# A quadrant swap in DRAM: 16 DMA engines that work on 16 neighbouring rows, or on rows 17 apart

## The chip, the cores and the metric

The kernel runs on one core of a Trainium2 chip. The time is that of the device for one execution, in microseconds (us). The input lies in DRAM, the output goes to DRAM, and both have 8192 x 8192 float32 elements, 268.44 MB each.

## The reference

```python
def reference(x: np.ndarray) -> np.ndarray:
    return np.fft.ifftshift(x)
```

With 8192 rows and columns this swaps quadrants. Output row r, column c is input row (r + 4096) mod 8192, column (c + 4096) mod 8192. Nothing is calculated: each half row of the output (4096 elements, 16 KB) is one contiguous half row of the input.

## The kernel before, in words

The kernel consists of DMAs from DRAM to DRAM and nothing else. No tile in on-chip memory is used, and no compute engine takes part. A DMA here is an instruction on one of two queues: that of SyncE (SP, `nc.sync`) and that of ScalarE (ACT, `nc.scalar`). It is described by three dimensions, the first of which has 16 entries, one for each of the core's 16 DMA engines (`ENGINES`, L9). In what follows "engine" means one of these 16.

`copy` (L26 to L32) issues one DMA. Its dimensions are `[[C, 16], [16 * C, 16], [1, hc]]`: engine e starts at row `row + e` and then takes every sixteenth row, 16 rows in all, half a row (16 KB) at a time. A row is 32 KB long, so at any moment the 16 engines are set to work on 16 neighbouring rows, 32 KB apart, and each engine goes on in steps of 512 KB. One DMA moves 256 half rows, 4 MB.

The loop (L35 to L38) goes over the rows in 32 blocks of 256. In each block SP's queue copies one half of the rows and ACT's queue the other half. Which half is SP's alternates from block to block. So each queue has 32 DMAs, and the two queues carry equal bytes. The program itself contains no wait between DMAs. Those that the profile shows are put in by the layer that turns the program into instructions.

Of the kernel before, what the change touches and what calls it, by code (L numbers as in the profile page):

```python
# [1 line left out]

# [4 lines left out]


ENGINES = 16  # L9


@with_exitstack
def kernel(
    ctx: ExitStack,
    tc: tile.TileContext,
    x: bass.AP,
    out: bass.AP,
):
    nc = tc.nc
    R, C = x.shape  # L20
    hr = R // 2
    hc = C // 2
    per = 16
    rows = ENGINES * per

    def copy(queue, row, h, step):  # L26

        dims = [[C, ENGINES], [step * C, per], [1, hc]]
        queue.dma_start(
            out=bass.AP(out.tensor, out.offset + row * C + h, dims),  # L30
            in_=bass.AP(x.tensor, x.offset + (row + hr) % R * C + hc - h, dims),
        )  # L32


    for n, row in enumerate(range(0, R, rows)):  # L35
        left = n % 2 == 0
        copy(nc.sync, row, 0 if left else hc, ENGINES)
        copy(nc.scalar, row, hc if left else 0, ENGINES)  # L38


# [1 line left out]
_INS = ['x']  # L42
_OUTS = [((8192, 8192), 'float32')]


def kernel(**inputs):
    import numpy as _np
    import concourse.bacc as _bacc
    import concourse.tile as _tile
    from concourse import mybir as _mybir  # L50
    from concourse.bass_utils import run_bass_kernel_spmd as _run

    nc = _bacc.Bacc("TRN2", target_bir_lowering=False, num_devices=1)  # L53
    arrays, args = {}, []
    for name in _INS:
        a = _np.ascontiguousarray(inputs[name])
        if a.dtype.kind in "iu":
            a = a.astype(_np.int64)
        arrays[f"in_{name}_dram"] = a
        args.append(nc.dram_tensor(f"in_{name}_dram", a.shape, _mybir.dt.from_np(a.dtype), kind="ExternalInput").ap())  # L60
    for i, (shape, dtype) in enumerate(_OUTS):
        dt = _mybir.dt.from_np(_np.dtype(dtype))
        args.append(nc.dram_tensor(f"out_{i}_dram", shape, dt, kind="ExternalOutput").ap())
    with _tile.TileContext(nc) as tc:
        kernel(tc, *args)
    r = _run(nc, [arrays], core_ids=[0])
    got = tuple(r.results[0][f"out_{i}_dram"] for i in range(len(_OUTS)))
    return got[0]
```

## Time and profile before

| What | Value |
|---|---|
| Median of 3 runs | 813.71 us (813.11 to 814.12) |
| Profiled execution: span from the first to the last instruction | 813.2 us |
| DMA issues, each of 4096 KB | 32 on SP's queue, 32 on ACT's |
| One issue on ACT's queue, min/median/max | 578 / 578 / 882 ns |
| One issue on SP's queue, min/median/max | 571 / 571 / 786 ns |
| From issue to landing, min/median/max | 25.3 / 101.1 / 104.6 us |
| Rate of reading in 100 to 800 us | 332 GB/s |

The profile covers one execution, and its span stands for the device time: 813.2 us lies inside the range of the three runs and 0.5 us from their median. The rate counts each byte once, though each is both read and written. The page counts packets, which are the single transfers an engine makes: 16,384 of them are half rows, and the 1,024 under 512 B are the 16 that each of the 64 DMAs ends with, one for each engine. "Share" in the table of queues is the time that the packets of a queue took, out of 16 engines for the whole span.

### The profile page before, as it was taken

The numbers are of one execution on the slowest core, as the hardware profiler recorded it, in microseconds if no ns is written. First come the engines' busy times: TensorE is split into PE (matmuls) and PEld (weight loads), VectorE is DVE, ScalarE is ACT, GpSimd is POOL, SyncE is SP. The second block draws the span as 40 slices with busy tenths as digits, with TensorE's granted clock in tenths as the row PEclk, the third lists the DMA queues.
The fourth block names the chain that finished last, engine by engine and source line by source line (L and its number), as shares of the span: only waits on it lengthen the run. The fifth ranks groups of instructions, "written<-read, shape, count | busy, mean of one in ns | idle before, by whom it ended". The sixth has DMA issues, their size and how long they took to land. (4 is left out here: it accounts for less than half of the span.)

```text
span 813.2 us, 109 instructions
## 1 busy us (share of the span) xinstructions
POOL 0.2 (0%) x4
## 2 busy tenths in 40 slices
POOL 0000000000000000000000000000000000000000
DMA  9999999999999999999999999999999999999998
GB/s 303 336 326 331 334 329 323 330 338 333 330 333 330 334 334 330 335 334 330 325 338 330 336 330 334 334 333 331 341 331 330 334 334 330 333 328 336 331 334 276
DMA packets 17408, 268.44 MB, mean 330 GB/s; under 512 B 1024, under 2 KB 1024, under 8 KB 1024
## 3 DMA queue, kind: packets, MB, share of 16 engines
q1 hardware_dynamic: 8704, 134.22, 50.4%
q10 hardware_dynamic: 8704, 134.22, 48.6%
HBM read 268.44 MB, written 268.44 MB: 660 GB/s over the span
## 5 line engine op out<-in xcount | busy, mean ns | idle before, releaser
L53 POOL MEMSET const-bfloat16-1.0<- 128x1 bf16 x1 | 0.1, 102 | 0.0
L53 POOL MEMSET const-uint8-127<- 128x1 uint8 x1 | 0.1, 101 | 0.0
L53 POOL MEMSET const-float32-0.0<- 128x1 f32 x1 | 0.1, 99 | 0.2 <-issue 0.2
L53 POOL MEMSET const-float32-1.0<- 128x1 f32 x1 | 0.1, 98 | 0.0
## 6 DMA issues: line engine op xcount, KB each, us to landing
out_dram<-in_x_dram SPq DMA_DIRECT2D x32, 4096.0 KB, 101.2
out_dram<-in_x_dram ACTq DMA_DIRECT2D x32, 4096.0 KB, 101.1
```

What stands on the lines that cost most here:

```text
L53: nc = _bacc.Bacc("TRN2", target_bir_lowering=False, num_devices=1)
```

## The change

The rows are cut into four parts: the upper and the lower 4096 rows, each with the left and the right half of the columns. In each part, SP's queue now copies a slanted band. Engine e starts 17 rows behind engine e - 1 in memory order (`(ENGINES + 1) * C`) and again walks in steps of 16 rows. So at each step the engines stand 17 rows (544 KB) apart, where they stood one row apart. A band takes 241 steps of 16 rows each (`last` = 4096 / 16 - 15). It is cut into seven DMAs of 32 steps and one of 17. That makes 32 DMAs on SP's queue: 28 of 8 MB and 4 of 4.25 MB.

The band leaves a triangle of rows at the start and at the end of each part, 120 half rows each. ACT's queue copies these. A DMA takes n neighbouring half rows (n from 1 to 15) and cuts each into 16 strips of 256 elements (1 KB), one for each engine. The DMAs of start and end alternate, with 15 - m and m + 1 half rows. So each pair has 16 half rows, and each part has 15 pairs. That makes 120 DMAs with 960 half rows (15.73 MB) and 960 strips for each engine.

In the program, all 32 DMAs of SP's queue are written first, and then all 120 of ACT's.

```diff
-    per = 16
-    rows = ENGINES * per
-
-    def copy(queue, row, h, step):
-
-        dims = [[C, ENGINES], [step * C, per], [1, hc]]
+    def copy(queue, row, col, dims):
         queue.dma_start(
-            out=bass.AP(out.tensor, out.offset + row * C + h, dims),
-            in_=bass.AP(x.tensor, x.offset + (row + hr) % R * C + hc - h, dims),
+            out=bass.AP(out.tensor, out.offset + row * C + col, dims),
+            in_=bass.AP(x.tensor, x.offset + (row + hr) % R * C + (col + hc) % C, dims),
         )
-    for n, row in enumerate(range(0, R, rows)):
-        left = n % 2 == 0
-        copy(nc.sync, row, 0 if left else hc, ENGINES)
-        copy(nc.scalar, row, hc if left else 0, ENGINES)
+    steps = 32
+    ahead = ENGINES - 1
+    strip = hc // ENGINES
+    last = hr // ENGINES - ahead
+    parts = [(row, h) for h in (0, hc) for row in (0, hr)]
+
+    for begin, h in parts:
+        for at in range(0, last, steps):
+            n = min(steps, last - at)
+            copy(
+                nc.sync,
+                begin + ENGINES * at,
+                h,
+                [[(ENGINES + 1) * C, ENGINES], [ENGINES * C, n], [1, hc]],
+            )
+
+    for begin, h in parts:
+        for m in range(ahead):
+            for row, n in (
+                (ENGINES * m + m + 1, ahead - m),
+                (ENGINES * (last + m), m + 1),
+            ):
+                copy(nc.scalar, begin + row, h, [[strip, ENGINES], [C, n], [1, strip]])
```

## The prediction

> **What bounds the kernel now.** I read the page first: the slices of the span, then the queues. There is nothing but DMA in it.
>
> ```profile
> span 813.2 us, 109 instructions
> DMA  9999999999999999999999999999999999999998
> GB/s 303 336 326 331 334 329 323 330 338 333 330 333 330 334 334 330 335 334 330 325 338 330 336 330 334 334 333 331 341 331 330 334 334 330 333 328 336 331 334 276
> DMA packets 17408, 268.44 MB, mean 330 GB/s; under 512 B 1024, under 2 KB 1024, under 8 KB 1024
> HBM read 268.44 MB, written 268.44 MB: 660 GB/s over the span
> ```
>
> The 16 engines are busy in every slice, and except in the first and the last the rate stays between 323 and 341 GB/s. So no wait of the program sets the time, only the rate at which bytes move. A half row takes 0.786 us on an engine: the queues' shares, 50.4% and 48.6%, are 99.0% of 16 x 813.2 us, over 16,384 half rows. Next I read the same view for the stretch from 100 to 800 us, to have the rate without start and end:
>
> ```profile
> DMA packets 15092, 232.59 MB, mean 332 GB/s; under 512 B 896, under 2 KB 896, under 8 KB 896
> q1 hardware_dynamic: 7545, 116.28, 50.7%
> q10 hardware_dynamic: 7547, 116.31, 49.0%
> ```
>
> At 332 GB/s, 268.44 MB take 808.6 us. The other 4.6 us are the start (nothing moves in the first 2 us) and the end (20 GB/s in the last 3.2 us). 808.6 + 4.6 = 813.2 us, the whole span. I work against this span; the median of the runs is 0.5 us more.
>
> Two more views tell how DMAs are kept in flight: the waits of SP's queue, and the landings of the instructions on the line that issues.
>
> ```profile
> SPq L29 <- DMA out_dram<-in_x_dram: 689.7, 28, 25.1
> ...
> L29 SPq DMA_DIRECT2D out_dram<-in_x_dram x32: 571/571/786, 0.7 to 709.0; - x32
> L29 ACTq DMA_DIRECT2D out_dram<-in_x_dram x32: 578/578/882, 0.7 to 713.9; - x32
> ...
> DMA to landing us min/median/max: 25.3/101.1/104.6
> ```
>
> Of SP's 32 DMAs, 28 wait for an earlier DMA: four go out at once, then one every 25 us. A landing after 101.1 us is four times that interval, so four are in flight on each queue and eight on both. An issue costs its queue 0.57 to 0.88 us. Eight in flight is plenty here, since the queues wait with 75 us of work in hand.
>
> **The change part by part.**
>
> *Rows 17 apart in place of 1.* The bytes are the same, and so is the size of SP's packets. What might change is how the DRAM takes them, and nothing in this trace shows rows 17 apart. The nearest rows bound it. At the fastest slice, 341 GB/s, 268.44 MB would take 787 us, and at the slowest inner one, 323, they would take 831 us. The queues give another hint. q1 and q10 carry the same packets, but q1's take 50.7 / 49.0 = 3.5% longer. Both work on the same rows shortly after each other, so this could be the price of being first at a row; if every half row paid q1's price, the rate would fall by 50.7 / 49.85 = 1.7%. Both bounds stay in the range. I take no change, 332 GB/s. The rate is even over the span, also across its middle, where the rows read change from lying 4096 behind the rows written to lying 4096 before them. That looks like one shared limit and not like a loss from where rows lie.
>
> *One queue in place of two for the bulk.* Before, every engine has work from two queues. Afterwards SP's queue alone carries 252.7 MB. The trace shows one queue alone only at the start: in the first 4 us, 46 half rows of q1 move, and their share (55.2% of 16 x 4 us) makes 0.768 us each, against 0.786 for the whole. So one queue is enough. Four DMAs of 32 half rows per engine in flight are twice the depth of before. Cost: nothing, covered by that depth. Should only one DMA be in flight, each of SP's 32 would expose a landing and a new issue, a few us each.
>
> *The strips.* 960 strips of 1 KB per engine. By bytes a strip takes 0.786 / 16 = 0.049 us. No packet of 1 KB is in the trace. The small ones there are the 1,024 at the DMAs' ends. The idle 1.0% of engine time is 130 us, of which the first 4 us (45% idle) and the last 8.2 us (43% idle) hold 85. If all of the other 45 us were theirs, a small packet would lose 0.044 us. So a strip costs 0.049 to 0.093 us, and all 960 cost 47 to 89 us per engine where by bytes 47 are due. I take the lower end while SP's packets run beside them, because the rate is then shared with the other engines' half rows.
>
> *When the strips run.* This is the step I expect to decide. The program writes no waits; before, they hold each DMA until one of eight places is free. I read these places as one ring of eight shared by both queues in the order of issue, rather than four for each queue. The trace of before can't tell these apart, since its queues alternate. If they are shared and both queues go out in turn, a DMA waits for the one eight places earlier. The first 32 strip DMAs then alternate with SP's 32 and run beside them. From then on, only ACT's are left, and every other one finds its place held by one of SP's last four: the 34th strip DMA waits for SP's 29th, the 36th for the 30th, the 38th for the 31st, the 40th for the 32nd and last. So 39 strip DMAs run beside SP's work and 81 behind its end. (Were all 32 of SP's counted first, only 7 would run beside it and 113 behind.)
>
> The sum: the first 39 hold 30 of part one (240 half rows), then four pairs (64) and one of 11, in all 315 half rows, 5.16 MB. Up to the end of SP's work, 252.71 + 5.16 = 257.87 MB move, in 776.7 us at 332 GB/s. The other 81 DMAs have 645 half rows, 10.57 MB, which at 332 GB/s would take 31.8 us. But they are small: 131 KB on average, one queue issues them, and an issue takes 0.578 us at its shortest and 0.882 at its longest, which gives 46.8 to 71.4 us. I take 0.60, near the median, since the long ones appear only in the first four, with both queues issuing: 48.6 us. Beside the issue, eight in flight cover 4.8 us of landing each. Total: 2.2 us start + 776.7 + 48.6 + 3.4 for the last landing and the end = **831 us**, 18 us over 813.2. That is all in the tail: 48.6 where 31.8 were due, and about 1 us of landing.
>
> A rule speaks against this tail more strongly. The Trainium skill, page "DMA: Bandwidth & Descriptors", section "Rules for kernel authors", says that many small transfers should be joined and that under 64 KB one pays mostly overhead; its table in "Bandwidth" has 138 GB/s at 64 KB, measured to on-chip memory one at a time. An estimate by that figure: 10.57 MB take 77 us, and the total is 859 us. No run here shows it.
>
> **The rivals.**
>
> *A: the strips flow beside SP's work to the end* (four places for each queue, or an order of issue that keeps the two in step). Each engine takes the queues in turn if the equal packets of q1 and q10 mean that (7545 and 7547), and SP has 964 half rows per engine to ACT's 960 strips. So they could end together. Then the time is 813.2 plus whatever strips cost above their bytes: nothing to 42 us, and I expect 0 to 5. For it: four in flight per queue fits the trace equally well. Against it: no view shows that a place belongs to a queue. Time 813 to 818.
>
> *B: the rate rises, and the kernel is faster.* Engines 17 rows apart would collide less in DRAM. For it: the spread of the slices up to 341, and 351 GB/s in one stretch of 5 us (785 to 790), show that the engines can go faster. Against it: no slice stays there. With the tail, 341 GB/s gives 257.87 MB in 756.2 us and 810 us in all; without a tail 787 + 4.6 = 792 us. At 351 it is 789 and 769 us. It decides from the point where the body gains the tail's 18 us, a rate 2.4% higher (340 GB/s); without a tail, from 0.3%. A sentence of the Trainium skill bears on how far this can go: "HBM Reference", section "Specifications", gives about 716 GB/s per domain, and the 660 here would by this estimate leave 750 us at best; no run here shows that limit.
>
> *C: the rate falls, too.* If rows 17 apart all pay q1's price, 776.7 becomes 790, and strips at 0.093 us make the tail 645 x 0.093 = 60 us and add 14 to the body. That is 870 us at the far end, with 850 in the middle.
>
> **How the numbers follow.** A difference under 0.2%, 1.6 us, is about what a measurement of this kernel can't tell from none. My forecast (tail, rate within about 1.5%) has 0.45, around 831 us, from 820 to 843. A has 0.14, half of it within 0.2%. B has 0.28, all faster. C has 0.13. So faster 0.28, same 0.07, slower 0.65 (0.45 + 0.07 + 0.13). For the range I leave out half of C beyond 852 and about a third of B, below 790: 790 to 852 us.
>
> **What would show it.** The tail: the last slices have packets on ACT's queue alone and a rate near 10.57 MB / 48.6 us = 217 GB/s, after some 779 us at 332. ACT's waits: a very long one, from about a quarter of the span to nine tenths, in which no strip is issued. The strips: packets under 2 KB on one queue, and the share of that queue over their number is the price of one. The rate: any stretch with SP's packets alone, against 332 GB/s. If that stretch is over 340, B holds; under 327, C. If the strips' issues are spread over the span, A holds and my step on the shared places is wrong.

## The result

The changed kernel takes **858.96 us** (median of 4 runs, 857.70 to 861.09). Beside it the kernel before takes 813.63 us. The ratio is **1.056 (95% interval 1.054 to 1.058)**: slower, as forecast, but by 45 us where 18 were forecast, and above the range of 790 to 852 us.

The page of the changed kernel, first its span, slices and packets, then its queues (packets, MB, share of the 16 engines' time):

```profile
span 859.3 us, 201 instructions
...
DMA  8578999999999899999999999999999999999996
GB/s 294 182 227 299 327 316 320 328 320 317 321 327 327 286 325 322 329 333 327 327 329 323 318 305 329 326 323 329 328 325 327 309 315 322 325 324 323 326 321 215
DMA packets 33217, 268.45 MB, mean 312 GB/s; under 512 B 2432, under 2 KB 17792, under 8 KB 17792
...
q1 hardware_dynamic: 15936, 252.71, 89.2%
q10 hardware_dynamic: 17280, 15.74, 6.7%
```

Before, no slice between the first and the last was under 323 GB/s. Now the second and third, from 21.5 to 64.5 us, have 182 and 227, and there are smaller dips, one in each quarter or so, and at the end. The shares turn this into a sum. One engine was busy for 99.0% of 813.2 us before, so idle for 8.1 us. Now it is busy for 95.9% of 859.3 us and idle for 35.2 us. The 46.1 us between the spans are made up of:

| Part, per engine | Before | After | Difference |
|---|---|---|---|
| 964 half rows, after the change on SP's queue alone, at 0.786 and 0.795 us | 757.7 us | 766.5 us | +8.8 us |
| Another 60 half rows, after the change 960 strips at 0.060 us | 47.2 us | 57.6 us | +10.4 us |
| Idle | 8.1 us | 35.2 us | +27.1 us |

So three fifths of the loss is time in which the engines have nothing to do. The busy time by stretch (start:end, length, POOL's busy time, clock, busy share of the 16 engines, GB/s) shows where the two largest parts of it lie:

```profile
21.50:33.00 11.50, 0.00 (x0) 1.00 0.68 229
33.00:51.00 18.00, 0.00 (x0) 1.00 0.42 125
51.00:64.50 13.50, 0.00 (x0) 1.00 0.91 293
310.00:430.00 120.00, 0.00 (x0) 1.00 1.00 328
846.00:859.30 13.30, 0.00 (x0) 1.00 0.48 150
```

From 21.5 to 51 us the idle shares make 11.5 x 0.32 + 18 x 0.58 = 14 us, and in the last 13.3 us they make 7 us. The other 14 us of the 35.2 lie mostly in the smaller dips and at the start. From 310 to 430 us SP's packets run alone, at 328 GB/s:

```profile
q1 hardware_dynamic: 2481, 39.34, 100.0%
```

That is under the 332 GB/s of before, but it is neither the 340 that the prediction named as the sign of rival B nor below the 327 that it named for C.

The waits of SP's queue and the order in time of what was issued between 20 and 90 us (start, length, queue, count) show who stands still in the first gap:

```profile
SPq L26 <- DMA out_dram<-in_x_dram: 423.5, 8, 80.3
...
22.36 62.70 ACTq L26 DMA_DIRECT2D out_dram<-in_x_dram  x43
51.21 56.34 SPq L26 DMA_DIRECT2D out_dram<-in_x_dram  x5
```

SP issues its first large DMA at 0.73 us, and it lands 31.9 us later. SP's second is issued only at 51.21 us, and meanwhile ACT issues strips. What holds it can be read in the program that the layer below builds from the kernel. I number all 152 DMAs in its order of issue; each holds one of eight places until it lands, and the right column is the wait that the program writes for it:

```
 1   ACT 1st          place 1
 2   SP  1st          place 2
 10  ACT 9th          place 2    waits for SP 1st
 42  SP  2nd          place 2    waits for ACT 33rd
 53  SP  3rd          place 5    waits for ACT 43rd
 60  ACT 51st         place 4    waits for SP 8th
 143 ACT 111th        place 7    waits for SP 32nd
```

The places are one ring of eight for both queues, as the prediction read them. The order is not what it took it for: 39 strip DMAs stand between SP's first and second. ACT's ninth needs the place of SP's first and stops until it lands. Then 24 more strip DMAs must be issued at some 0.65 us each until SP's second gets its place, and by then SP's queue has been empty since 33 us. A second kind of wait follows at the end of each part. The 51st, 71st, 91st and 111th strip DMAs wait for SP's last DMA of their part (the 8th, 16th, 24th and 32nd), although it holds another place than theirs. Their rows lie within its range of rows, but no half row is copied by both; why the layer asks for this wait isn't shown. So no strip is issued from 703 to 849 us, and the last ten strip DMAs run alone behind SP's last one.

### The profile page after: what moved, and what is told of

Read it like the earlier page. It is cut to its first block, busy times and chain, and to the rows that moved or that the text cites. A ratio compares the mean times of both kernels' runs of the same rounds, so it can differ in the third digit from the quotient of the medians.

```text
span 859.3 us, 201 instructions
## 1 busy us (share of the span) xinstructions
POOL 0.2 (0%) x4
```

## The experiments

They ran in five groups on four chips. The kernel before took 822 to 823 us there, so I compare ratios to it within a group, and rates in the middle of a run (from 100 to 700 us). Kernels that leave the triangles out move 0.941 of the bytes.

### Bands alone: rows 17 and one apart, one and two queues

The changed kernel without its second loop, and the same with one edit:

```diff
-                [[(ENGINES + 1) * C, ENGINES], [ENGINES * C, n], [1, hc]],
+                [[C, ENGINES], [ENGINES * C, n], [1, hc]],
```

The two-queue versions have `steps = 16` and give the left half to SP and the right half to ACT, for the lower rows the other way round.

> The changed kernel without its 120 strip DMAs: SP's 32 DMAs alone, rows 17 apart; the triangles (960 of 16,384 half rows) are left out. Each engine has 964 half rows. The half rows took 0.786 us each before and 0.7945 us in the changed kernel. If only the order of issue and the strips cost time (theory O), they are back at 0.786 and the time is 964 x 0.786 + 8.2 = 766 us. If rows 17 apart cost (theory R) or one queue costs (theory Q), it stays at 0.7945 and the time is 774 us. If rows 17 apart gain and the strips hide it (theory G), it is under 760 us.

> The same 32 DMAs on SP's queue with the engines one row apart (the step from engine to engine is C in place of 17 C); the last 240 rows of each part are left out, so the bytes are the same. Theory O: 766 us. Theory R: 766 us, 8 us below its counterpart with rows 17 apart. Theory Q: 774 us, the same as its counterpart.

> The bands with rows 17 apart, cut into DMAs of 16 steps that go to SP's and ACT's queue in turn, as before the change; the triangles are left out. Theory O: 766 us. Theory R: 774 us. Theory Q: 766 us.

> The kernel before, short of the same 960 half rows: rows one apart, DMAs of 16 steps on both queues in turn. All theories: 813.7 less 60 half rows of 0.786 us per engine, 766.5 us.

| Bands alone | One queue | Two queues |
|---|---|---|
| Rows 17 apart | 801.80 us, 0.976 (0.971 to 0.981) | 797.70 us, 0.971 (0.966 to 0.975) |
| Rows one apart | 777.22 us, 0.946 (0.942 to 0.951) | 774.03 us, 0.942 (0.939 to 0.945) |

Theory R holds here, with three times the 8 us that it expected. Rows 17 apart cost 3.1% with either number of queues. One queue instead of two is 0.4 to 0.6% slower, which the overlapping intervals can't tell from nothing. In the middle of the one-queue runs, 17 apart first:

```profile
DMA packets 11927, 189.12 MB, mean 315 GB/s; under 512 B 384, under 2 KB 384, under 8 KB 384
```

```profile
DMA packets 12451, 197.45 MB, mean 329 GB/s; under 512 B 400, under 2 KB 400, under 8 KB 400
```

The same bytes, packets and queue, and 4% in the rate. That is more than the 3.1% in time, since the profiled execution was the slowest of four with rows 17 apart and the fastest with rows one apart.

### The order of issue repaired, and engines far apart

The strips go to SP's queue, four DMAs behind each large one, and each part's strips beside another part:

```diff
+    strips = strips[2 * ahead :] + strips[: 2 * ahead]
     for begin, h in parts:
         for at in range(0, last, steps):
...
+            for _ in range(4):
+                if strips:
+                    row, col, k = strips.pop(0)
+                    copy(nc.sync, row, col, [[strip, ENGINES], [C, k], [1, strip]])
```

The version one apart has `[[C, ENGINES], ...]` and takes its strips from the last 240 rows of each part. The last run exchanges two dimensions of the kernel before:

```diff
-        dims = [[C, ENGINES], [step * C, per], [1, hc]]
+        dims = [[per * C, ENGINES], [C, per], [1, hc]]
```

> The changed kernel once more, so that the three kernels beside it can be compared with it on one chip: 1.056 times the kernel before, as in its first runs.

> The changed kernel with its strips on SP's queue, four strip DMAs behind each of SP's large ones and each part's strips beside another part, so that no large DMA waits for work that is not nearly done. Rows stay 17 apart, strips stay 1 KB; only the order of issue is repaired. Theory O (the gaps in issue cost their full idle time): the 27 us of added idle go, ratio 1.056 - 0.033 = 1.023. Theory R (rows 17 apart cost 3%, and the gaps partly hide that): 0.976 for the bands as measured alone plus 960 strips of 0.049 to 0.059 us, 0.058 to 0.070, so a ratio of 1.034 to 1.046.

> The same order and the same number and size of strips, but the engines one row apart and the strips in the last 240 rows of each part. What is left against the kernel before is the price of the strips and of one queue. Bands alone were 0.946; with strips of 0.049 to 0.059 us, 0.058 to 0.070 more: a ratio of 1.004 to 1.016. If strips of 1 KB cost nothing above their bytes, 1.00. Theory R also wants it 0.03 below its counterpart with rows 17 apart; theory O wants the two equal.

> The kernel before with engine and step exchanged in its DMAs: engine e takes 16 rows that follow each other, and the engines are 16 rows (512 KB) apart. The same DMAs move the same rows in the same order on the same queues. If engines far apart cost by themselves (theory R, wide), it loses what rows 17 apart lose, about 3%: 1.03. If the loss belongs to the walk in steps of 512 KB from places 544 KB apart (theory R, narrow), it is the same as before, 1.00. Theory O: 1.00.

| Kernel | Time | Ratio |
|---|---|---|
| The changed kernel again | 866.45 us | 1.054 (1.050 to 1.058) |
| Strips behind the bands, rows 17 apart | 834.15 us | 1.015 (1.011 to 1.018) |
| Strips behind the bands, rows one apart | 831.85 us | 1.015 (1.008 to 1.021) |
| Engines 16 rows apart, steps of one row | 821.81 us | 0.999 (0.996 to 1.002) |

The order repaired gives 32 us back, more than either theory had. The shares of the queues, first of the changed kernel again (862.8 us in the profile), then with the strips behind (833.3 us), show where from:

```profile
q1 hardware_dynamic: 15936, 252.71, 89.3%
q10 hardware_dynamic: 17280, 15.74, 6.8%
```

```profile
q1 hardware_dynamic: 33216, 268.45, 98.3%
```

Idle time falls from 3.9% to 1.7%, from 34 to 14 us per engine. So 20 us come from the waits, and the rest from packets that take less time in all: by their records a half row takes 0.776 us on average in place of 0.799, while a strip takes 0.073 in place of 0.060. With rows 17 apart and the strips behind, the stretch of the first gap and the middle read:

```profile
21.50:64.50 43.00, 0.00 (x0) 1.00 0.99 325
100.00:700.00 600.00, 0.00 (x0) 1.00 0.99 325
```

The gap is gone. What is left, 12 us, is the price of the strips and the single queue together: rows one apart with the same strips cost as much. That speaks against theory R, whose 3% is nowhere to be seen in this pair. And engines 512 KB apart lose nothing that could be measured, so wide distances don't cost by themselves.

### The contradiction, on one chip

The bands' pairs and the strips' pairs had run on different chips. The same kernels again on one, with the strips alone beside them:

> The bands with rows 17 apart alone on SP's queue, a second time, triangles left out. In their first run the bands alone were 3.1% slower with rows 17 apart than with rows one apart (0.976 against 0.946 of the kernel before), but with strips between them the two spacings were equal (1.015 and 1.015), and those two pairs ran on different chips. If the strips make the difference (theory M, mixing), the ratio is 0.976 again. If the chip makes it (theory C), it is some 0.95 on a chip where strips behind the bands give 1.015.

> The bands with rows one apart alone on SP's queue, a second time, the same bytes left out. Both theories: 0.946 of the kernel before.

> Rows 17 apart with the strips on SP's queue behind the large DMAs, a second time. Theory M: 1.015 again, however the bands alone come out. Theory C: if the bands alone with rows 17 apart are slow on this chip, this is slow too, 1.035 to 1.045; if they are not, 1.015.

> Only the 120 strip DMAs on ACT's queue; the bands (15,424 of 16,384 half rows) are left out. If the issue sets their pace, as the prediction had it for the tail: 120 x 0.60 + 6 = 78 us. If the bytes do, 15.73 MB at 330 GB/s + 6 = 54 us. If each waits for landings with eight in flight, more than 78 us.

Bands alone: 804.33 us with rows 17 apart, 0.977 (0.972 to 0.982), against 776.13 us, 0.942 (0.938 to 0.946). Strips behind the bands, 17 apart: 834.16 us, 1.013 (1.009 to 1.017). So it isn't the chip: rows 17 apart cost 3.7% in the bands alone, and nothing measurable in the kernels with strips behind them.

The strips alone took 84.11 us (one run). The 120 issues go from 0.7 to 78.5 us, one every 0.654 us:

```profile
L26 ACTq DMA_DIRECT2D out_dram<-in_x_dram x120: 598/612/682, 0.7 to 78.5; - x120
...
DMA to landing us min/median/max: 2.4/2.9/3.6
```

They land in 2.9 us, well inside the 5.2 us of eight places, so the issue sets the pace, as the prediction had it for a tail. Its 0.60 us left out the gap from one issue to the next.

### What makes rows 17 apart slow

The trace has the 16 landings of each DMA, one for each engine. In the bands alone with rows 17 apart, they lie within 1.3 us on average, from the first to the last DMA: the engines march in step, less than two half rows apart. With rows one apart this spread grows from 1.6 us in the first quarter of the DMAs to 2.7 us in the last, while the rate rises from 321 (15 to 100 us) to 330 GB/s (500 to 700 us). With strips behind, it is 5 to 6 us. That led to theory M, that marching in step is what costs. Four runs, with these edits to the bands alone, 17 apart:

```diff
+    for k in (8, 4, 2):
+        copy(
+            nc.sync,
+            hr + ENGINES * (ENGINES - 2 * k) + ENGINES - k,
+            hc,
+            [[C, k], [ENGINES * C, k], [1, hc]],
+        )
```

```diff
-    steps = 32
+    steps = 8
```

```diff
-                [[(ENGINES + 1) * C, ENGINES], [ENGINES * C, n], [1, hc]],
+                [[(2 * ENGINES + 1) * C, ENGINES], [ENGINES * C, n], [1, hc]],
```

For 33 rows apart, `ahead` is 30 as well; for 15 the first step is `(ENGINES - 1) * C`.

> The bands alone with rows 17 apart, after three small DMAs that only the first 8, 4 and 2 entries of the first dimension take part in (8, 4 and 2 half rows each, out of the triangles). If the DMA engines with these entries have that work and the others don't, engines start their bands up to 14 half rows (11 us) after others. The triangles' other half rows are left out. Theory M (17 apart is slow only while the 16 engines march in step; what sets them off against each other removes it): the rate in the middle is that of rows one apart, 327 to 330 GB/s, and the time some 777 to 790 us with the late engines' end. Theory D (slow because too much is in flight) and theory S (17 apart is slow in any case): 313 to 317 GB/s, 803 to 815 us.

> The bands alone with rows 17 apart in DMAs of 8 steps in place of 32, so that eight in flight are 64 half rows per engine, no more than two large DMAs. Triangles left out. Theory D: as fast as rows one apart, 0.944 of the kernel before. Theories M and S: 0.977, as with 32 steps.

> The bands with the engines 33 rows apart, steps of 16 rows as before; the triangles are larger, and 904 half rows per engine are left of 1,024. Marching in step, engine e then is at row 16 (k + 2 e) + e. If any distance between engines that march in step costs what 17 rows cost, the ratio is 0.883 x 0.977 / 0.941 = 0.916. If it is the one block of 16 rows more for each row within the block that collides (theory H), 33 is free of it: 0.883 x 0.944 / 0.941 = 0.885.

> The bands with the engines 15 rows apart, steps of 16 rows; 964 half rows per engine as with 17. Marching in step, engine e is at row 16 (k + e) - e. Theory H (the row within the block of 16 and the block's number together choose a place in the DRAM, and here one goes down as the other goes up): it collides at least as much as 17, 0.977 or more. If 17 rows are slow for another reason: anything from 0.944.

| Bands alone | Time, ratio | Middle, GB/s | Spread of landings |
|---|---|---|---|
| 17 apart (above, second run) | 804.33 us, 0.977 | 315 | 1.3 us |
| 17 apart, engines set off | 799.19 us, 0.972 (0.970 to 0.975) | 321 | 8.4 us, constant |
| 17 apart, steps of 8 | 807.35 us, 0.984 (0.979 to 0.989) | 316 | 1.4 us |
| 15 apart | 799.83 us, 0.972 (0.967 to 0.976) | 321 | 1.2 us |
| 33 apart (0.883 of the bytes) | 732.48 us, 0.894 (0.889 to 0.898) | 326 | 1.3 us |
| One apart (above, second run) | 776.13 us, 0.942 | 327 | 1.6 to 2.7 us |

A smaller depth in flight (theory D) doesn't help. Theory M is half right: engines that were set off stay so, in four groups, and about half of the loss in rate is gone. But marching in step isn't enough, since 33 rows apart marches as strictly and is nearly free in its rate (326 GB/s); in time it is 0.9 points above the 0.885 that no loss would give, where the loss of 17 rows would give 3.1. Theory H wanted 33 free, which it nearly is, and 15 at least as bad as 17. It came out a little better, but the intervals of 15 and 17 overlap and they ran on different chips, so H isn't settled.

The changed kernel bears on this, too. It has stretches in which SP's packets run almost alone, and there the spread differs: 1.5 us on average from 112 to 231 us, 2.6 from 320 to 436, and 4.6 from 524 to 641. The rates of these stretches:

```profile
100.00:230.00 130.00, 0.00 (x0) 1.00 0.99 322
300.00:435.00 135.00, 0.00 (x0) 1.00 1.00 327
505.00:640.00 135.00, 0.00 (x0) 1.00 1.00 327
```

Against the 332 GB/s of before, that is a loss of 3.0% at the smallest spread and of 1.5% at the other two. In a second execution, on another chip, the spread was 2.2 to 3.3 us and the rate 322 to 324, where the kernel with engines 16 rows apart has 329. So once the engines are out of step, 17 rows cost less than in the bands alone even while no strip runs, but not nothing. All this fits a loss that depends on the distance and on who is where at the same time. A collision in the DRAM would be such a loss, but no run here shows one; the cause stays open.

### The sharing of places alone

One word of the changed kernel:

```diff
-                copy(nc.scalar, begin + row, h, [[strip, ENGINES], [C, n], [1, strip]])
+                copy(nc.gpsimd, begin + row, h, [[strip, ENGINES], [C, n], [1, strip]])
```

and, beside it, the kernel before with the engines set off:

> The changed kernel with one word changed: the strip DMAs are issued on GpSimd's queue. The order of issue of all 152 DMAs stays as it was, but in the program built for it the strips now hold eight places of their own and SP's DMAs wait for SP's DMAs only. If the shared places made the gaps (theory P), the slices from 21 to 64 us run at over 300 GB/s and the ratio is 1.015 to 1.035 in place of 1.054. If the gaps have another cause (the order itself, or the strips' own pace), it stays at 1.05. If GpSimd issues slowly, the strips end late, but SP's bands still flow.

> The kernel before, after three small DMAs (8, 4 and 2 half rows on the first 8, 4 and 2 entries) that copy 84 half rows of the last block twice and set engines off by up to 14 half rows. Theory M, also for rows one apart (the rate rose from 321 to 330 GB/s in the bands alone while the engines drifted apart): the rate is above that of the kernel before from the start, 333 to 337 GB/s, and the time is 0.99 to 1.00 of it with 4 to 11 us for the additional rows. If rows one apart lose nothing in step: the same rate, 1.005 to 1.013.

The strips on a third queue take 843.32 us, 1.027 (1.022 to 1.031). The first gap and the end:

```profile
21.50:64.50 43.00, 9.09 (x17) 1.00 1.00 326
...
821.00:841.60 20.60, 5.43 (x10) 1.00 0.33 119
```

The order of issue is unchanged and the gap is gone, so theory P holds: it was the shared places, together with this order. The tail is still there, and longer, because the last ten strip DMAs still wait for SP's last one. On this queue the strips go in fewer and larger packets (6,528 for the same bytes, the DMAs' ends included), so the price of a strip isn't compared.

The kernel before with its engines set off takes 832.99 us, 1.013 (1.009 to 1.016), at 326 to 330 GB/s. That is no gain in rate. But the trace shows that only half of the work was set off: the landings of a DMA on SP's queue spread over 21 us on average, and those on ACT's queue over only 3.1 us. So this run says little on whether rows one apart lose something to marching in step. The additional time of 10 us fits the additional rows and the late engines; the run doesn't separate them. No version here beats the kernel before.

## Why the prediction was wrong, step by step

- **What bounds the kernel** was right. Where nothing starves the engines, the rate stays at 315 to 332 GB/s in every kernel with half rows.
- **When the strips run** is the step that failed. It took the shared places for what they are but assumed that "both queues go out in turn", so that 39 strip DMAs run beside SP's work and 81 behind it, a tail of 48.6 us. In the trace 110 run before SP's last DMA has landed and 10 behind it, and in the last 13.3 us the engines idle for 7 us. What the sum had no term for is the other side of sharing: SP waits for ACT's strips too, and its queue runs empty near the start, which makes 14 us of idle time by itself. The waits of the profile before could not show this; a long wait of the large queue was never priced, only one of ACT's. All added idle time is 27.1 us in the trace. The order repaired gives back 32 us, of which 20 are idle time, and the places separated give back 22 us (0.027 of 823 us).
- **The direction** was right, but not for the forecast reason: the tail that was to hold the whole loss holds 7 of the 35.2 us of idle time, and the rest of the loss comes from terms that the sum had at nothing.
- **The strips** were bounded well (0.049 to 0.093 us; 0.060 measured), but taken at the lower end. In the changed kernel they cost 10.4 us above their bytes. On SP's own queue, with the order repaired, a strip takes 0.073 us.
- **Rows 17 apart** were taken at no change, with 1.7% as the far end. Alone they cost 3.1 to 3.7%, outside the rows it was bounded by. In the changed kernel SP's packets are only 1.1% longer, 8.8 us. The landings of an SP DMA spread over 3.1 us there on average (1.2 to 5.3), so engines out of step may be the reason; that isn't shown. What the prediction drew from q1 and q10 isn't borne out: in the kernel with engines 16 rows apart the two queues have 49.4 and 49.7%, at the same rate.
- **One queue for the bulk** was priced at nothing; the 0.4 to 0.6% measured, 3 to 5 us, lie within the intervals.
- **The issue** at 0.60 us was a little low; alone it is 0.654 us.
- **The rivals:** A was nearer on where the strips run, since 110 of the 120 run beside SP's work, but its places for each queue and its 813 to 818 us are out. B's gain appears in no run. C named two of the three prices, a lower rate and dearer strips. Its 850 to 870 us hold the measured time, but only with a tail of 60 us that isn't there.

The estimate of 859 us by the Trainium skill's figure ("DMA: Bandwidth & Descriptors", "Bandwidth") meets the time, but by chance: it put 77 us into a tail that takes 13.3. Strips alone move at 200 GB/s (from 5 to 75 us), where that page of the Trainium skill has 138 at 64 KB.

The same page of the Trainium skill, section "Latency and other measured facts", has copies slow down at row pitches that are large powers of two and advises to pad them by a few KB. Here the measurement goes the other way at the distance between engines: exactly 512 KB apart loses nothing (0.999), and 544 KB apart loses 3.7%. The measurement decides for this kernel; the two differ in more than the pitch.

## What to carry to other kernels

Where DMAs of very different size share a ring of completion places, a large one can stand behind dozens of small ones, and the queue that carries the bulk runs dry: read each queue's waits and the order of issue after a change, not only the bytes. Put leftovers behind the large DMAs on the same queue, or on a queue with places of its own (1.015 and 1.027 of the kernel before, in place of 1.054). Compare access patterns alone, without what runs beside them, and then again with it: here one pattern cost 3.7% alone and nothing measurable in company.

## What the runs showed that was not expected

- Engines that carry equal work march in step by themselves, within 1.3 us over 800 us, for some distances (15, 17 and 33 rows) and drift for others (1 and 16). Set off once by three small DMAs, they keep their distance: with rows 17 apart, the landings of a DMA spread over 8.2 to 8.6 us on average in each quarter of the run.
- An issue can block its queue for long. With several DMAs of 32 steps in flight, SP's issue instruction itself takes up to 53.7 us in the changed kernel, where 0.57 is the shortest. The profile doesn't list that time as a wait (minimum, median and maximum in ns):

```profile
L26 SPq DMA_DIRECT2D out_dram<-in_x_dram x32: 571/778/53696, 0.7 to 754.4; - x32
```
